# A transformer layer's seven-product matmuls: at each change of the resident operand, two blocks in turn through seven products instead of one block of eight

## The chip, the cores and the metric

One core of a Trainium2 chip runs the whole kernel. The metric is device time in microseconds (us), the median of three runs; before the change it is 2656.38 us (2653.74 to 2657.7). The engines are named as in the profile: PE (TensorE) with its weight loads PEld, DVE (VectorE), ACT (ScalarE), POOL (GpSimd), and SP (SyncE), which only issues DMAs.

## The reference: what is computed

One layer over x (2048 tokens, width 1024), all in float32:

```python
u = rms_norm(h, g_mix_pre);  z = u @ w_in            # 1024 x 2816
y = concat(swa_with_sinks(...), hgrn2(...)) @ w_out  # 1024 x 1024
h = h + rms_norm(y, g_mix_post)
y = cross_attention(rms_norm(h, g_x_pre), rms_norm(mem, g_mem), wq, wk, wv, wo)
h = h + rms_norm(y, g_x_post)
u = rms_norm(h, g_ffn_pre)
y = (silu(u @ w_gate) * (u @ w_up)) @ w_down         # 1024 x 2816 x 1024
h = h + rms_norm(y, g_ffn_post)
```

The large matrix products carry the time. Cross-attention reaches them as two of them: the query and key weights are folded into one 1024 x 1024 matrix (`qk_d`), value and output weights into another (`vo_d`).

## The kernel before, in words

**One product.** A float32 operand is kept as a rounded part and a rest (hi, lo: `split2`, L873 to L880: ACT or POOL writes hi, DVE writes lo = raw - hi). A product of a piece S (128 columns) with a resident tile T (512 columns) over `nk` slices of 128 is three matmuls for each slice, hi*hi, hi*lo, lo*hi (`products`, L1002 to L1004): 12 matmuls at nk = 4, 9 at nk = 3.

**One block.** A block is a 2x2 product of blocks: A (four pieces of 128 columns, loaded as two `sraw` tiles and split into S tiles by `streamed`) times B (four quarters, kept split as T tiles by `resident`, so that every block of a job uses the same T). It is done in one of two ways.

- `seven` (kind "s"): Strassen's way in Winograd's form. The T tiles of steps 1, 2 and 3 are quarters of B; those of steps 5, 7, 6 and 4 are differences and sums of quarters. Three S pieces of the seven are also sums (`combine`, L977, four DVE additions for a block). Three PSUM banks are used, x, y and z: x takes the products 1, 6, 7 and 4 one upon the other and is read in between (`copy`, L1017, into a `part` tile, after 1 and after 6; z is copied after 5); the outputs are x, y or z plus a copy.
- `eight` (kinds "p" and "q"): the eight plain products in four steps of two (T tiles 1, 2, 8, 3), no sums and no copies, but a T tile 8 that `seven` doesn't need.

The order of the steps stands in `STEPS` and how many S pieces each step takes in `TAKES`.

**Jobs.** A job is one B with a row of blocks; `phases` runs all jobs as one stream. The first one (`in_first`: w_in, half the tokens, 11 blocks: q, p, nine s) runs before the attention and recurrence sections, which use other code. `jobs` (L1242 on) lists the others: w_out (8 blocks), qk (8), vo (8), the FFN's gate and up products for the first half of the tokens and for the second (22 blocks each; here B is `u_d`, the normalised activations, and A the weights), and three parts of w_down (8 blocks each; nk = 3, 4, 4). At a change of job the T tiles change. `kinds` says which blocks are plain: in w_out and the first FFN job the first and the last one, in all others the last one, save that the very last block is "s": nine plain blocks in all, of which eight run behind another job or in front of one and one (w_out's first) is the start of the second part.

**The T tiles' turn.** Seven slots hold T tiles. `queue` orders them by first use; `half` starts loading half a tile (into `row` tiles of 128 x 1024, of which there are 9 for everything) when a slot's last use is past, and `split` writes the halves two products later. For qk, vo, the second FFN job and w_down the combined T's (5, 7, 6, 4) are prepared one job earlier by `combined` (L924) and stored to DRAM (`qk_s` and so on); for w_out and the first FFN job DVE combines them on the spot (L906).

**Around it.** S pieces are made two products ahead (`upto`). A block's `follow` goes on for about ten products behind it: for vo it normalises (L1439), adds the residual by an accumulating DMA issued from POOL (`add`, L1348), stores h2, squares (L1319), normalises again (L1450), transposes on PE (L1237, L1238) and stores `u_d`. Each takes one step after each product. Every tile comes from a pool with a fixed number of buffers: S 5, `raw` (the sraw tiles) 3 in the first job and 4 later, `sum` 3, `part` 3, PSUM banks for products 6. A scheduler places the instructions of each engine by its own cost estimate; each engine then runs its list in order and waits on semaphores.

Of the kernel before, what the change touches and what calls it, by code (L numbers as in the profile page):

```python
# [48 lines left out]
class Layer:  # L49
# [144 lines left out]
    def mix(self):  # L194
        tc, I = self.tc, self.I
        kw = dict(reuse_waits="tile")
        with contextlib.ExitStack() as left:
# [5 lines left out]
            with (  # L203
                tc.tile_pool(name="t1", bufs=3, **kw) as self.ts,
                tc.tile_pool(name="t2", bufs=3, **kw) as self.tb,
                tc.tile_pool(name="s1", bufs=2, side="right", **kw) as self.st_pool,
                contextlib.ExitStack() as at,
            ):
                self.banks(at, "ps1", **MOST)
                self.raws = 3  # L210
                u = self.in_first()
# [32 lines left out]
            with (  # L244
# [6 lines left out]
                self.raws = 4  # L251
# [264 lines left out]
    def in_block(self, ca, cb, beside, get, between):  # L516
# [20 lines left out]
        def out(i, j, a, b):  # L537
# [14 lines left out]
            else:  # L552
                self._n += 1
                t = self.st_pool.tile([P, 512], F32, tag="part", name=f"th_{self._n}", bufs=3)
# [315 lines left out]
    STEPS = {"s": (1, 5, 6, 3, 7, 2, 4), "p": (1, 2, 8, 3), "q": (1, 2, 8, 3)}  # L870
    TAKES = {"s": (1,) * 7, "p": (2, 2, 0, 0), "q": (4, 0, 0, 0)}
# [83 lines left out]
    def streamed(self, load, nk, kind, engine=None):  # L955
# [18 lines left out]
        def combine(a, b, op):  # L974
            self._n += 1
            t = self.st_pool.tile([P, 4, P], F32, tag="sum", name=f"sum_{self._n}", bufs=3)[:, :nk, :]
# [29 lines left out]
    def seven(self, S, T, nk, out, addend):  # L1006
# [6 lines left out]
        def copy(ps, i, j):  # L1013
            self._n += 1
            t = self.st_pool.tile([P, 512], F32, tag="part", name=f"part_{self._n}", bufs=3)
# [67 lines left out]
    def phases(self, jobs, first, prologue=None):  # L1083

        steps = [(n, i, p) for n, job in enumerate(jobs) for i, b in enumerate(job[2])
                 for p in self.STEPS[b[0]]]
        takes = [c for job in jobs for b in job[2] for c in self.TAKES[b[0]]]
        need = list(itertools.accumulate(takes)) + [sum(takes)] * 2  # L1090
# [5 lines left out]
        queue = sorted(uses, key=lambda k: (uses[k][0] - (5 if k[1] == 7 and jobs[k[0]][3] is None else 0), k))  # L1096
# [73 lines left out]
        blocks = [b for job in jobs for b in job[2]]  # L1170
        streams, ready, made = [], [], [0]

        def stream(at):
            if at < len(blocks):
                streams.append(blocks[at][1](blocks[at][0]))
                next(streams[-1])

        def upto(count):
            while made[0] < count:
                s = next(streams[0], None)  # L1180
                if s is None:
                    streams.pop(0)
                    continue
                ready.append(s)
# [9 lines left out]
        for i in range(2):  # L1194
            upto(need[i])
# [3 lines left out]
        at = 0  # L1199
        self.last = {}  # L1200
        for _, nk, bl, _, beside in jobs:
            for i, (kind, _, out, follow, addend) in enumerate(bl):
                stream(at + 1)
                after += [f() for f in beside.get(i, ())]
                run = (self.seven(ready, Ready(), nk, out, addend) if kind == "s" else
                       self.eight(ready, Ready(), nk, out, addend, kind == "q"))
                for q in range(len(self.STEPS[kind])):
                    next(run)
                    self.mark()
                    upto(need[g + 2])  # L1210
                    for _ in range(1 if kind == "s" else 2):
# [10 lines left out]
                after.append(follow())  # L1222
                at += 1
# [20 lines left out]
    def jobs(self):  # L1244
# [21 lines left out]
        def kinds(blocks, n=0):  # L1266
            return [("p" if i < n or i == len(blocks) - 1 else "s",) + b for i, b in enumerate(blocks)]
# [19 lines left out]
        jobs = [(w_out, 4, kinds([self.mixed_block(n) for n in range(0, NT, 2)], 1), None, {2: [qk_s[1]]}),  # L1287
# [302 lines left out]
```

## Time and profile before

| | |
|---|---|
| median of 3 runs | 2656.38 us (2653.74, 2656.38, 2657.7) |
| span of the profiled execution | 2652.4 us; the page has no other time of it |
| matmul instructions | 12329 |
| DVE, ACT, POOL busy | 1714.9, 1240.2, 485.2 us |
| 0 to 265 us | first job (w_in, half the tokens) |
| 265 to 815 us | w_in for the rest, attention, recurrence, folding of the cross-attention weights |
| 815 to 1010, to 1190, to 1375 us | w_out, qk, vo |
| 1375 to 2220 us | the two FFN jobs |
| 2220 to 2652 us | w_down in three parts |

The profile is one execution. A row of a timeline has start, duration, engine, line, operation, out<-in and shapes; in brackets stands how long the engine had been idle before and what released it. In a table by windows each engine has its busy time and, in brackets, its number of instructions; PEclk is the clock granted to PE. The bounds of the jobs above are read from the first and last rows of each job's tiles, to some 10 us, since neighbouring jobs overlap.

### The profile page before, as it was taken

The numbers are of one execution on the slowest core, as the hardware profiler recorded it, in microseconds if no ns is written. First come the engines' busy times: TensorE is split into PE (matmuls) and PEld (weight loads), VectorE is DVE, ScalarE is ACT, GpSimd is POOL, SyncE is SP. The second block draws the span as 40 slices with busy tenths as digits, with TensorE's granted clock in tenths as the row PEclk, the third lists the DMA queues.
The fourth block names the chain that finished last, engine by engine and source line by source line (L and its number), as shares of the span: only waits on it lengthen the run. The fifth ranks groups of instructions, "written<-read, shape, count | busy, mean of one in ns | idle before, by whom it ended". The sixth has DMA issues, their size and how long they took to land.

```text
span 2652.4 us, 34824 instructions
## 1 busy us (share of the span) xinstructions
PE 2568.9 (97%) x12329; PEld 2145.1 (81%) x12329; DVE 1714.9 (65%) x2701; ACT 1240.2 (47%) x2604; POOL 485.2 (18%) x675
## 2 busy tenths in 40 slices
PE   7999999999988999999989999999999999999998
PEld 6877888888986877888878888888888888888886
DVE  7675578877545657777666655556666656564656
ACT  5463366655433556555564333344333334353543
POOL 4240344322432323223310000000000000001022
PEclk9999999999999999999999999999999999999999
DMA  5435655445877998676893633253566435576988
GB/s 183 144 130 165 191 156 159 131 140 171 233 234 222 276 296 266 210 238 176 220 307 126 192 120 95 80 182 127 168 198 211 162 108 171 173 232 173 264 214 215
DMA packets 405102, 494.48 MB, mean 186 GB/s; under 512 B 20416, under 2 KB 311232, under 8 KB 404928
## 3 DMA queue, kind: packets, MB, share of 16 engines
q1 hardware_dynamic: 394272, 453.46, 53.3%
q0 software_dynamic: 10656, 38.80, 8.3%
q8 instruction: 97, 1.59, 0.2%
q14 instruction: 77, 0.63, 0.1%
HBM read 333.85 MB, written 158.33 MB: 186 GB/s over the span
## 4 chain that ended last, share of the span: by engine, by line
PE 75%; DMA 10%; issue 7%; DVE 4%; POOL 3%; ACT 2%; SPq 0%; POOLq 0%; DVEq 0%; ACTq 0%
PE psm L1002 20%; PE psm L1004 20%; PE psm L1003 20%; PE psg L160 2%; PE psg L159 2%; PE psg L158 2%; PE pss L1237 1%; DMA row<-y_d 1%; DMA row<-in_w_out_dram 1%; DMA u_d<-row 1%; DMA raw<-in_wv_x_dram 1%; DMA raw<-in_wo_x_dram 1%; DVE wlo L143 1%; DMA row<-in_x_dram 1%; DMA pair<-in_x_dram 0%
## 5 line engine op out<-in xcount | busy, mean ns | idle before, releaser
L1002 PE MATMUL psm<-T,S 128*128 128x512 f32 x2699 | 1049.2, 393 | 19.9 <-ACT part L1017 6.9
L1003 PE MATMUL psm<-T,S 128*128 128x512 f32 x2699 | 1054.7, 391 | 5.7 <-DVE T L880 5.7
L1004 PE MATMUL psm<-T,S 128*128 128x512 f32 x2699 | 1046.4, 392 | 0.7 <-DVE S L880 0.6
L1002 PEld LDWEIGHTS psm<-T,S 128*128 128x128 f32 x2699 | 509.3, 189 | 132.3 <-ACT part L1017 8.2
L1003 PEld LDWEIGHTS psm<-T,S 128*128 128x128 f32 x2699 | 509.3, 189 | 111.8 <-DVE T L880 7.4
L1004 PEld LDWEIGHTS psm<-T,S 128*128 128x128 f32 x2699 | 509.2, 189 | 108.9 <-DVE S L880 3.1
L880 DVE TENSOR_TENSOR S<-sraw,S 128x512 fp32r<-128x512 f32 (+1 forms) x320 | 222.9, 703 | 213.3 <-ACT S L877 195.9
L877 ACT ACTIVATE S<-sum 128x512 fp32r<-128x512 f32 (+1 forms) x310 | 186.4, 619 | 342.5 <-PE psm L1004 244.3
L880 DVE TENSOR_TENSOR S<-sum,S 128x512 fp32r<-128x512 f32 (+1 forms) x368 | 248.5, 686 | 55.4 <-ACT S L877 35.7
L1017 ACT ACTIVATE part<-psm 128x512 f32<-128x512 f32 x270 | 160.0, 597 | 245.9 <-PE psm L1004 227.9
L1348 POOL DMA_DIRECT2D row<-y_d x28 | 25.7, 918 | 1127.4 <-DVE row L1521 1033.9
L877 ACT ACTIVATE S<-sraw 128x512 fp32r<-128x512 f32 (+1 forms) x273 | 168.0, 616 | 122.7 <-PE psm L1004 102.8
L880 DVE TENSOR_TENSOR T<-row,T 128x1024 fp32r<-128x1024 f32 (+1 forms) x122 | 144.2, 1195 | 63.8 <-ACT T L877 63.6
L158 PE MATMUL psg<-u,whi 128*128 128x512 f32 x352 | 141.3, 401 | 1.6 <-POOL whi L142 1.6
L160 PE MATMUL psg<-u,wlo 128*128 128x512 f32 x352 | 139.6, 397 | 0.9 <-DVE wlo L143 0.9
L159 PE MATMUL psg<-u,whi 128*128 128x512 f32 x352 | 139.4, 396 | 0.0
L877 ACT ACTIVATE T<-row 128x1024 fp32r<-128x1024 f32 x122 | 122.3, 1028 | 33.2 <-DVE row L906 17.9
L1319 ACT ACTIVATE junk<-row 128x512 f32<-128x512 f32 x160 | 99.9, 626 | 79.1 <-DVE row L1341 28.4
L879 POOL TENSOR_SCALAR S<-sum 128x512 fp32r<-128x512 f32 x58 | 50.2, 865 | 209.8 <-PE psm L1004 159.9
L977 DVE TENSOR_TENSOR sum<-sraw,sraw 128x512 f32<-128x512 f32 (+1 forms) x92 | 64.0, 696 | 32.0 <-DMA sraw<-h1t_d 8.7
L143 DVE TENSOR_TENSOR wlo<-raw,whi 128x1024 fp32r<-128x1024 f32 x46 | 60.3, 1311 | 36.1 <-POOL whi L142 36.1
L1472 DVE TENSOR_TENSOR row<-psm,part 128x512 f32<-128x512 f32 x63 | 41.7, 688 | 59.3 <-PE psm L1004 59.2
(332 smaller groups left out, 3622.0 us busy)
## 6 DMA issues: line engine op xcount, KB each, us to landing
sraw<-in_w_gate_dram SPq DMA_DIRECT2D x44, 512.0 KB, 3.9
sraw<-in_w_up_dram SPq DMA_DIRECT2D x44, 512.0 KB, 4.0
hid_d<-row SPq DMA_DIRECT2D x44, 512.0 KB, 2.6
h_d<-row SPq DMA_DIRECT2D x32, 512.0 KB, 5.8
y_d<-row SPq DMA_DIRECT2D x32, 512.0 KB, 3.1
sraw<-hid_d SPq DMA_DIRECT2D x32, 512.0 KB, 5.3
row<-h_d POOLq DMA_DIRECT2D x30, 512.0 KB, 6.5
row<-u_d SPq DMA_DIRECT2D x30, 512.0 KB, 6.3
```

The source lines that it names most:

```text
L143: (lo_engine or nc.vector).tensor_tensor(lo, raw, f32(hi), ALU.subtract)
L158: nc.tensor.matmul(ps, ah, bh, start=(i == 0), stop=False)
L159: nc.tensor.matmul(ps, ah, bl, start=False, stop=False)
L160: nc.tensor.matmul(ps, al, bh, start=False, stop=(i == n - 1))
L877: self.nc.scalar.activation(hi, raw, AF.Copy)
L880: self.nc.vector.tensor_tensor(lo, raw, f32(hi), ALU.subtract)
L977: nc.vector.tensor_tensor(t, a, b, op)
L1002: nc.tensor.matmul(ps, s[:, 0, k, :], t[:, 0, k, :], start=st, stop=False, **kw)
L1003: nc.tensor.matmul(ps, s[:, 0, k, :], t[:, 1, k, :], start=False, stop=False, **kw)
L1004: nc.tensor.matmul(ps, s[:, 1, k, :], t[:, 0, k, :], start=False, stop=sp, **kw)
L1017: nc.scalar.activation(t, ps, AF.Copy)
L1319: self.nc.scalar.activation(junk, a, AF.Square, scale=float(D) ** -0.5, accum_out=to)
```

## The change

- A new kind "d": two neighbouring blocks go through the seven steps in turn, product by product (step 1 of the one, step 1 of the other, step 2 of the one, ...), so that each T is used twice before the next is needed. All jobs from w_out on begin and end with such a pair, save w_out's start (still one "p" block) and the end of the last job (still "s").
- The order of the seven steps is 1, 2, 5, 6, 7, 3, 4 for "s" and "d" (was 1, 5, 6, 3, 7, 2, 4), and the S pieces are made in that order.
- T tile 7, where it isn't prepared a job earlier, is fetched directly ahead of 6 (was five places early).
- Pools: `raw` 6 (was 4) and `sum` 5, `part` 4 (were 3) from the second part on. To make room in SBUF `dynamic_dma_scratch_size=2048` is given, the bytes of each partition kept for the descriptors of DMAs issued from POOL.

```diff
-    STEPS = {"s": (1, 5, 6, 3, 7, 2, 4), "p": (1, 2, 8, 3), "q": (1, 2, 8, 3)}
+    STEPS = {"s": (1, 2, 5, 6, 7, 3, 4), "d": (1, 2, 5, 6, 7, 3, 4), "p": (1, 2, 8, 3), "q": (1, 2, 8, 3)}
...
-                self.raws = 4
+                self.raws, self.parts, self.sums = 6, 4, 5
...
         yield made(a11, "A")
+        yield made(a12, "A")
         s1 = combine(a21, a22, ALU.add)
         yield made(s1, "P")
         s2 = combine(s1, a11, ALU.subtract)
         yield made(s2, "A")
+        yield made(combine(a11, a21, ALU.subtract), "P")
         yield made(combine(a12, s2, ALU.subtract), "A")
-        yield made(combine(a11, a21, ALU.subtract), "P")
-        yield made(a12, "A")
         yield made(a22, "P")
...
+                members = (i, i + 1) if job[2][i][0] == "d" else (i,)
...
-        queue = sorted(uses, key=lambda k: (uses[k][0] - (5 if k[1] == 7 and jobs[k[0]][3] is None else 0), k))
+        def turn(k):
+            if k[1] == 7 and jobs[k[0]][3] is None:
+                return uses[k[0], 5 if first else 6, 0][0] - 0.5, k
+            return uses[k][0], k
+
+        queue = sorted(uses, key=turn)
...
+            for q in range(len(self.STEPS[kind])):
+                for i in members:
+                    next(runs[i])
                     self.mark()
-                    upto(need[g + 2])
+                    upto(g + 2)
...
-        def kinds(blocks, n=0):
-            return [("p" if i < n or i == len(blocks) - 1 else "s",) + b for i, b in enumerate(blocks)]
+        def kinds(blocks, first="dd", last="dd"):
+            middle = "s" * (len(blocks) - len(first) - len(last))
+            return [(k,) + b for k, b in zip(first + middle + last, blocks)]
...
-    nc = _bacc.Bacc("TRN2", target_bir_lowering=False, num_devices=1)
+    nc = _bacc.Bacc("TRN2", target_bir_lowering=False, num_devices=1, dynamic_dma_scratch_size=2048)
```

More of the change, by code (lines that the diff above doesn't have):

```diff
@@ L975, in combine @@
             self._n += 1
-            t = self.st_pool.tile([P, 4, P], F32, tag="sum", name=f"sum_{self._n}", bufs=3)[:, :nk, :]
+            t = self.st_pool.tile([P, 4, P], F32, tag="sum", name=f"sum_{self._n}", bufs=self.sums)[:, :nk, :]
             nc.vector.tensor_tensor(t, a, b, op)
@@ L1014, in copy @@
             self._n += 1
-            t = self.st_pool.tile([P, 512], F32, tag="part", name=f"part_{self._n}", bufs=3)
+            t = self.st_pool.tile([P, 512], F32, tag="part", name=f"part_{self._n}", bufs=self.parts)
             if addend is None:
```

84 lines of the change are left out of this document (47 added, 37 removed).

## The prediction

> **What bounds the kernel now.** First the head of the page: span, engines, the clock, the chain that ended last.
>
> ```profile
> span 2652.4 us, 34824 instructions
> PE 2568.9 (97%) x12329; PEld 2145.1 (81%) x12329; DVE 1714.9 (65%) x2701; ACT 1240.2 (47%) x2604; POOL 485.2 (18%) x675
> PE 75%; DMA 10%; issue 7%; DVE 4%; POOL 3%; ACT 2%; SPq 0%; POOLq 0%; DVEq 0%; ACTq 0%
> ```
>
> PE is busy 97% of the span and makes up 75% of the chain; DVE, next, is at 65%. So time is saved by fewer matmuls or by shorter waits of PE. The span is all that the page has of the profiled execution; the median of the runs, 2656.4 us, is 4.0 above it. I reckon changes on the span and add them to 2656.4.
>
> Second the table by windows, where PE is not full (PE, PEld, DVE, ACT, POOL, then PEclk, DMA share, GB/s).
>
> ```profile
> 800.00:850.00 50.00, 41.53 (x174) 31.66 (x173) 22.73 (x23) 18.52 (x33) 8.37 (x9) 0.96 0.88 257
> 1000.00:1050.00 50.00, 44.36 (x203) 36.45 (x202) 38.93 (x53) 34.39 (x71) 15.39 (x23) 0.93 0.84 261
> 1150.00:1200.00 50.00, 49.49 (x239) 41.17 (x238) 40.96 (x66) 33.50 (x68) 11.00 (x14) 1.00 0.79 255
> 1350.00:1400.00 50.00, 42.17 (x170) 32.73 (x169) 32.89 (x35) 28.77 (x52) 5.19 (x11) 0.86 0.91 291
> 1700.00:1750.00 50.00, 50.00 (x222) 41.42 (x221) 25.60 (x39) 17.48 (x31) 0.00 (x0) 1.00 0.31 96
> ```
>
> In the FFN (1700) PE never rests and the clock is 1.00. It loses time where the resident operand changes: 800 to 850 (w_out begins), around 1000 (w_out to qk), 1350 to 1400 (vo to FFN). The last has 170 PE instructions where a full window has 222: 52 short. What one is worth, from two matmuls of a stretch without a gap, 39 apart in PE's order:
>
> ```profile
> 1599.81 0.39 PE L1004 MATMUL psm<-T,S 128*128 128x512 f32 x1
> 1608.65 0.39 PE L1004 MATMUL psm<-T,S 128*128 128x512 f32 x1
> ```
>
> 8.84 / 39 = 0.2267 us (the 0.39 is a latency, it overlaps the next). So 1350 to 1400 loses 52 x 0.2267 = 11.8 us, and 1000 to 1050 some 4.5 (19 short, and its transposes are shorter than a matmul). Third, PE's timeline at these places, with the idle time before a row and its releaser:
>
> ```profile
> 842.39 0.50 PE L1003 MATMUL psm<-T,S 128*128 128x512 f32 x1 [1.02 <-DVE T L880]
> 845.19 0.50 PE L1002 MATMUL psm<-T,S 128*128 128x512 f32 x1 [1.35 <-ACT T L877]
> 849.80 0.80 PE L1003 MATMUL psm<-T,S 128*128 128x512 f32 x1 [4.11 <-DVE T L880]
> ...
> 1003.21 1.06 PE L1237 MATMUL pss<-ident,row 128*128 128x128 f32 x8 [1.03 <-DMA row<-in_x_dram]
> 1014.37 0.90 PE L1237 MATMUL pss<-ident,row 128*128 128x128 f32 x3 [4.62 <-ACT row L1238]
> ...
> 1189.97 0.50 PE L1002 MATMUL psm<-T,S 128*128 128x512 f32 x1 [0.51 <-ACT part L1017]
> ...
> 1385.08 0.80 PE L1002 MATMUL psm<-T,S 128*128 128x512 f32 x1 [5.28 <-ACT T L877]
> 1386.46 0.79 PE L1003 MATMUL psm<-T,S 128*128 128x512 f32 x1 [0.58 <-DVE T L880]
> 1387.47 0.63 PE L1002 MATMUL psm<-T,S 128*128 128x512 f32 x1
> 1387.90 0.63 PE L1003 MATMUL psm<-T,S 128*128 128x512 f32 x1
> 1389.78 0.79 PE L1002 MATMUL psm<-T,S 128*128 128x512 f32 x1 [0.82 <-ACT row L1474]
> ```
>
> The waits are for the T tiles themselves (L877, L880), or for a copy that waits behind other work. After the 5.28 us gap matmuls start 0.43 apart (1387.47, 1387.90), twice 0.2267: the clock is halved, so 7.7 us idle become 11.8. Behind the gap at 1385 the chain shows a store and a load of u_d in series:
>
> ```profile
> 1366.44 12.38 DMA u_d<-row
> ...
> 1378.89 6.66 DMA row<-u_d
> ```
>
> **The change, part by part.** *Matmuls.* Eight plain blocks go. Seven of them have nk = 4 and give up one product of 12 matmuls, one has nk = 3 and gives up 9: 7 x 12 + 9 = 93. The built order confirms it: 8568 product matmuls where there were 8661. 93 x 0.2267 = **21.1 us**, on PE, the path. Nothing covers it.
>
> *What DVE gets for it.* The rows for the pieces:
>
> ```profile
> L880 DVE TENSOR_TENSOR S<-sum,S 128x512 fp32r<-128x512 f32 (+1 forms) x368 | 248.5, 686 | 55.4 <-ACT S L877 35.7 <-POOL S L879 17.9
> L977 DVE TENSOR_TENSOR sum<-sraw,sraw 128x512 f32<-128x512 f32 (+1 forms) x92 | 64.0, 696 | 32.0 <-DMA sraw<-h1t_d 8.7 <-DMA sraw<-in_w_in_dram 8.3 <-issue 3.4
> L1521 DVE TENSOR_TENSOR row<-psm,part 128x512 f32<-128x512 f32 x66 | 45.0, 688 | 35.5 <-PE psm L1004 35.5
> L880 DVE TENSOR_TENSOR T<-row,T 128x1024 fp32r<-128x1024 f32 (+1 forms) x122 | 144.2, 1195 | 63.8 <-ACT T L877 63.6
> L906 DVE TENSOR_TENSOR row<-row,row 128x1024 f32<-128x1024 f32 x16 | 19.6, 1225 | 15.5 <-DMA row<-in_w_out_dram 13.2 <-DMA row<-u_d 2.1
> L1439 DVE SCALAR_TENSOR_TENSOR row<-row,q_r,g 128x1024 f32<-128x1024 f32 x16 | 20.2, 1303 | 6.4 <-POOL q_r L1334 6.4
> L1450 DVE SCALAR_TENSOR_TENSOR row<-row,q_r,extra 128x1024 f32<-128x1024 f32 x16 | 20.0, 1282 | 7.2 <-POOL q_r L1334 3.7 <-DMA u_d<-row 3.5
> L1398 DVE TENSOR_REDUCE x_mx<-row 128x2 f32<-128x512 f32 x21 | 14.3, 679 | 0.1
> L1410 DVE TENSOR_SCALAR row<-row,mc 128x256 f32<-128x256 f32 x64 | 18.5, 354 | 0.3
> ```
>
> By count of instructions, DVE gets 24 more S splits, 32 more sums and 24 more outputs, at 0.69, and 16 fewer T splits at 1.2 (T tile 8 goes): 80 x 0.69 - 16 x 1.2 = +36 us over the kernel. ACT gets 24 more copies and as many S halves, less 16 T halves. Over all that is beside PE. At the changes it isn't spread. A seven-product block costs DVE 7 splits + 4 sums + 3 outputs = 14 x 0.69 = 9.7 us; a vo block adds 2 x 1.30 + 2 x 1.28 (14.8), a w_out block 2 x 1.30 (12.3), a qk block 4 x 0.68 + 8 x 0.35 (15.2); gate and up, with their product, average 11.0. A new set of T costs 14 x 1.2 = 16.7, and 8 x 1.22 = 9.8 more where DVE combines. Two pairs around a change are 28 products, 28 x 12 x 0.2267 = 76.2 us of PE. DVE's work in them: w_out to qk 24.5 + 30.4 + 16.7 = 71.6 (94%), qk to vo 30.4 + 29.6 + 16.7 = 76.7 (101%), vo to FFN 29.6 + 22.1 + 16.7 + 9.8 = 78.2 (103%). Before, with one plain block before the change (and one behind it for the FFN), the same count gives 85%, 92% and 82%. By this the pairs cost at least 0.5 us at qk to vo and 2.0 at vo to FFN. The FFN's and w_down's own changes stay under 80%: 0, hidden under PE.
>
> *When it is due.* Against that stands the order. A pair uses each T for two products, so a new T is due every 5.4 us and not every 2.7, and its slot was freed a whole pair before. I added up, in the built orders, the DVE work that stands between the S pieces of two products, less PE's time for the products between: the largest excess. At w_out's start 36.0 us before and 24.9 now; w_out to qk 14.9 and 7.6; qk to vo 12.1 and 9.3; vo to FFN 20.3 (28.5 of DVE against 8.2 of PE) and 19.0 (over 43 us of PE). Before, 12.1 went with one wait of 0.51 (1189.97), 14.9 with 4.5 lost, 20.3 with 11.8. So I take: w_out to qk -2 (half of the 4.5, for the waits there name a DMA and a copy, not T; ends -4.5 and +3.1, if its 7.6 is uncovered); qk to vo +0.5 (ends 0 and +8.8); vo to FFN 0, its excess being the same (ends -11.8 and +6.7, 18.5 uncovered for 11.8).
>
> *Order of the steps.* At w_out's start T5 and T6 are due one product (2.7 us) later, as step 2 now stands before 5 and its T is there. Of the waits 1.02, 1.35 and 4.11 at 842 to 850 that takes **2.7** (ends 0 and -6.5). In the new order 6 and 7 follow each other in the same bank, with a copy between. In the built order mostly 22 to 24 matmuls (5 us) of the next block stand between them, more than the copy needs, so 0; were they neighbours, each of the 63 single blocks behind the first job would pay a wait like the last one of the kernel, below (0.88, 55 us together). Only at the end of the first job two products meet in one bank with no matmul between, where two stood:
>
> ```profile
> 260.93 0.47 PE L1002 MATMUL psm<-T,S 128*128 128x512 f32 x1 [0.42 <-DVE pair L543]
> ...
> 2640.42 0.47 PE L1002 MATMUL psm<-T,S 128*128 128x512 f32 x1 [0.88 <-DVE row L1521]
> ```
>
> 0.88 for 0.42: **+0.5**.
>
> *Pools, DMAs.* More raw, sum and part tiles only lift waits: a pair holds up to four part tiles at once, two copies for each block, which is what there is. T tile 8 goes with 18 loads of T, four of them at vo to FFN, whose DMA share is 0.91. I take 0; what it may give there is within the ends above. The scratch for POOL's DMAs: most at once are four, by their issues and landing time:
>
> ```profile
> 2605.28 0.95 POOL L1348 DMA_DIRECT2D row<-h_d  x1 [1.62 <-DVE row L1563]
> 2607.08 0.86 POOL L1348 DMA_DIRECT2D row<-h_d  x1 [0.85 <-DVE row L1563]
> 2607.68 1.17 POOL L1348 DMA_DIRECT2D row<-y_d  x1
> 2609.58 0.86 POOL L1348 DMA_DIRECT2D row<-y_d  x1 [0.74 <-ACT row L1525]
> ...
> q0 software_dynamic: 10656, 38.80, 8.3%
> ...
> row<-h_d POOLq DMA_DIRECT2D x30, 512.0 KB, 6.5
> ```
>
> A row of this queue is 10656 / 74 issues = 144 packets, 9 on each of 16 engines, so four are 36. I take 0; if the smaller ring made one wait for another's landing, 6.5 us at each such place, mostly beside w_down, where POOL has nothing else.
>
> Sum: -21.1 - 2.7 - 2 + 0.5 + 0 + 0.5 = -24.8; 2656.4 - 24.8 = **2632 us**.
>
> [...]
>
> **Rivals.** *A, the changes get smooth.* For it: each of the four excesses falls, and four loads fewer where DMA is at 0.91. Then w_out to qk gives 4.5, vo to FFN keeps its 2.0 of overflow and gives 9.8: -21.1 - 2.7 - 4.5 + 0.5 - 9.8 + 0.5 = -37, 2619 us. Against it: DVE at 101 and 103%.
>
> *B, row tiles at vo to FFN.* The last two vo blocks now end together and hold 4 y and 4 u rows, 8 of the 9 buffers, when the FFN's T's and outputs want theirs. The pair of rows above (12.38 + 6.66) is such a row coming free. For it: that is what ended the 5.28 gap; against: T's are fetched earlier than the u rows are taken. Once more it is 19.0 us, with the halved clock some 23: -24.8 + 23, 2655 us, no difference.
>
> *C, slower: DVE becomes the bound at the three changes.* Place: w_out to qk, qk to vo, vo to FFN. Price: the excesses uncovered, 7.6 + 9.3 + 18.5 = 35.4 us idle, by the 11.8 / 7.7 of 1385 54 with the halved clock, less 16.8 lost there now: +37. With -21.1 - 2.7 + 0.5 it is +14, 2670 us. It decides from where the three changes lose 23 us more than now. For it: 94 to 103%; against: the excess fell, and before, at 1150 to 1200, DVE's 40.96 of 50 us left PE 49.49.
>
> *D, nothing is saved*, because the pairs are pulled apart or the matmuls stay: excluded by the count of 8568.
>
> **How the numbers follow.** Forecast (2625 to 2645) 0.48; A (below 2625) 0.18; B (2645 to 2662) 0.18; C (above 2662) 0.14; 0.02 elsewhere. The measurement can tell 0.2%, 5.3 us, from no change. Faster, below 2651.1: 0.48 + 0.18 + half of B and the rest, 0.76; the same, to 2661.7: 0.10; slower: 0.14. Range: from the middle of A to the upper part of B, 2614 to 2657, which leaves C and the ends out.
>
> **What would show it.** In the profile after: 2668 matmuls on each of L1002 to L1004's lines for psm<-T,S, and PE busy some 20 us less. At w_out's start a last wait of 1 to 2 us in place of 4.11. The windows of the changes at 210 PE instructions or more and PEclk 1.00 speak for A; waits of PE on DVE T or DVE S at all three changes, DVE at 45 of 50 us, for C; a wait there that ends with a load of u_d behind a store, for B. I am wrong in the main if new waits of PE show within the FFN or w_down, which I cost at nothing.

## The result, and the profile after

The changed kernel takes 2650.72 us (median of 20 runs, 2643.26 to 2655.48) against 2656.59 us (20 runs, 2649.47 to 2665.44): a ratio of **0.9979, 95% interval 0.9970 to 0.9988**, 5.6 us less by the ratio. The forecast was 24.8 us less, 2632 us; the range, 2614 to 2657, holds the time. So some 19 us of the forecast gain are missing.

The head of the page of the changed kernel (span and engines) and one of the three lines of the products' matmuls:

```profile
span 2653.7 us, 34559 instructions
PE 2548.9 (96%) x12236; PEld 2126.5 (80%) x12236; DVE 1747.7 (66%) x2765; ACT 1241.9 (47%) x2624; POOL 488.0 (18%) x675
...
L1002 PE MATMUL psm<-T,S 128*128 128x512 f32 x2668 | 1039.3, 394 | 43.3 <-ACT part L1017 13.2
```

2668 instead of 2699, and PE is busy 20.0 us less (2568.9 before): the matmuls went as forecast. But the span isn't shorter, so PE's idle time grew by as much and 1.3 us more. This execution took 2655.48 us, the longest of the 20; a second profile, of run e8 below, is of one of 2647.06 us (span 2645.3). What both show I take for the kernel's, and the rest for scatter. The table by windows of the first (columns as in the prediction):

```profile
850.00:900.00 50.00, 36.32 (x142) 28.37 (x141) 36.50 (x42) 22.83 (x45) 13.75 (x19) 0.80 0.73 191
...
1150.00:1200.00 50.00, 50.00 (x230) 41.51 (x230) 42.01 (x70) 34.05 (x75) 13.97 (x19) 1.00 0.62 200
...
1350.00:1400.00 50.00, 41.62 (x183) 33.52 (x182) 42.47 (x50) 31.21 (x61) 13.45 (x16) 0.94 0.93 291
...
1700.00:1750.00 50.00, 50.00 (x222) 41.39 (x222) 28.08 (x44) 17.14 (x30) 0.00 (x0) 1.00 0.23 75
```

Inside the FFN PE is as full as before, and at 1150 to 1200, where DVE has 42 of 50 us, too. The new hole is 850 to 900, at the start of w_out: 142 instructions, clock 0.80 (before, that window had 227). PE's timeline there, and behind vo, with the idle time ahead of a row:

```profile
820.34 0.79 PE L1002 MATMUL psm<-T,S 128*128 128x512 f32 x1 [5.80 <-POOL S L879]
859.85 0.79 PE L1002 MATMUL psm<-T,S 128*128 128x512 f32 x1 [7.50 <-ACT T L877]
866.23 1.97 PE L1257 MATMUL pss<-ident,row 128*128 128x128 f32 x8 [4.64 <-DMA row<-in_x_dram]
...
954.10 0.76 PE L1002 MATMUL psm<-T,S 128*128 128x512 f32 x1 [4.10 <-DVE row L1361]
...
1344.32 0.50 PE L1002 MATMUL psm<-T,S 128*128 128x512 f32 x1 [2.36 <-ACT S L877]
...
1391.83 0.50 PE L1002 MATMUL psm<-T,S 128*128 128x512 f32 x1 [2.48 <-ACT part L1017]
1396.41 0.80 PE L1004 MATMUL psm<-T,S 128*128 128x512 f32 x1 [3.84 <-DVE S L880]
```

To see where the time went I measure each job in PE's timeline from the start of its first product matmul to the start of the next job's, and the last part of w_down to the start of the last product matmul. Where a job ends is found by counting: w_out has 684 product matmuls (696 before), qk and vo 672 (684), the FFN jobs 1848 (1872, 1860), w_down 504, 672, 672 (513, 684, 672). The first row goes from the span's start to the first matmul of w_in for the second half of the tokens, the second from there to w_out. All in us:

| | before | changed, 1st profile | 2nd profile | forecast change | change, 2nd |
|---|---|---|---|---|---|
| first job | 265.6 | 268.9 | 265.0 | +0.5 | -0.5 |
| to w_out's first product | 550.9 | 551.5 | 547.6 | 0 | -3.3 |
| w_out | 187.6 | 199.0 | 198.7 | -5.4 | **+11.2** |
| qk | 178.9 | 172.7 | 172.1 | -4.7 | -6.9 |
| vo | 169.2 | 173.1 | 172.5 | -2.2 | **+3.3** |
| FFN 1 | 441.6 | 434.7 | 436.8 | -5.4 | -4.9 |
| FFN 2 | 421.6 | 418.9 | 418.9 | -2.7 | -2.7 |
| w_down, first two parts | 271.3 | 266.6 | 266.6 | -4.8 | -4.8 |
| w_down, third part | 156.3 | 159.5 | 158.2 | 0 | **+1.9** |

(The forecast column is the prediction's sum laid out by job, 2.72 us for each block of 12 matmuls. Of the kernel before there is one profile; run e12 below, which differs from it in the scratch alone, has the same times to 2.1 us.) In FFN 2 and the first parts of w_down, where the matmuls are all that the sum changes, the forecast is right to 0.1 us. The loss stands in w_out with what leads to it (13 us off), vo (5.5 us) and the last part of w_down (2 to 3 us).

### The profile page after: what moved, and what is told of

Read it like the earlier page. It is cut to its first block, busy times and chain, and to the rows that moved or that the text cites. A ratio compares the mean times of both kernels' runs of the same rounds, so it can differ in the third digit from the quotient of the medians.

```text
span 2653.7 us, 34559 instructions
## 1 busy us (share of the span) xinstructions
PE 2548.9 (96%) x12236; PEld 2126.5 (80%) x12236; DVE 1747.7 (66%) x2765; ACT 1241.9 (47%) x2624; POOL 488.0 (18%) x675
## 4 chain that ended last, share of the span: by engine, by line
PE 73%; DMA 11%; DVE 6%; issue 3%; POOL 3%; ACT 2%; SPq 0%; POOLq 0%; DVEq 0%; ACTq 0%
PE psm L1002 20%; PE psm L1004 20%; PE psm L1003 20%; PE psg L160 2%; PE psg L159 2%; PE psg L158 2%; DMA row<-in_x_dram 1%; PE pss L1257 1%; DVE S L880 1%; DMA row<-u_d 1%; DMA row<-in_w_down_dram 1%; DMA z<-in_w_out_dram 1%; DMA row<-qk_s 1%; DVE T L880 1%; POOL whi L142 1%
## 5 line engine op out<-in xcount | busy, mean ns | idle before, releaser
L1002 PEld LDWEIGHTS psm<-T,S 128*128 128x128 f32 x2668 | 504.2, 189 | 155.6 <-ACT part L1017 16.5
L1004 PEld LDWEIGHTS psm<-T,S 128*128 128x128 f32 x2668 | 503.2, 189 | 117.0 <-DVE S L880 12.5
L1003 PEld LDWEIGHTS psm<-T,S 128*128 128x128 f32 x2668 | 504.1, 189 | 105.8 <-DVE T L880 2.5
L877 ACT ACTIVATE S<-sum 128x512 fp32r<-128x512 f32 (+1 forms) x336 | 206.9, 619 | 342.9 <-PE psm L1004 331.7
L880 DVE TENSOR_TENSOR S<-sraw,S 128x512 fp32r<-128x512 f32 (+1 forms) x312 | 211.4, 684 | 227.6 <-ACT S L877 207.6
L880 DVE TENSOR_TENSOR S<-sum,S 128x512 fp32r<-128x512 f32 (+1 forms) x400 | 274.3, 689 | 69.3 <-ACT S L877 57.5
L1017 ACT ACTIVATE part<-psm 128x512 f32<-128x512 f32 x294 | 173.3, 593 | 170.3 <-PE psm L1004 168.2
L1339 ACT ACTIVATE junk<-row 128x512 f32<-128x512 f32 x160 | 99.7, 625 | 112.8 <-DMA row<-in_x_dram 35.1
L880 DVE TENSOR_TENSOR T<-row,T 128x1024 fp32r<-128x1024 f32 x106 | 127.2, 1205 | 33.4 <-ACT T L877 33.0
L877 ACT ACTIVATE T<-row 128x1024 fp32r<-128x1024 f32 x106 | 108.1, 1029 | 59.2 <-DVE row L906 32.5
L1501 DVE TENSOR_TENSOR part<-psm,part 128x512 f32<-128x512 f32 x66 | 45.4, 688 | 63.4 <-PE psm L1004 63.3
```

The lines of the kernel that those rows point to most:

```text
L877: self.nc.scalar.activation(hi, raw, AF.Copy)
L880: self.nc.vector.tensor_tensor(lo, raw, f32(hi), ALU.subtract)
L1002: nc.tensor.matmul(ps, s[:, 0, k, :], t[:, 0, k, :], start=st, stop=False, **kw)
L1003: nc.tensor.matmul(ps, s[:, 0, k, :], t[:, 1, k, :], start=False, stop=False, **kw)
L1004: nc.tensor.matmul(ps, s[:, 1, k, :], t[:, 0, k, :], start=False, stop=sp, **kw)
L1017: nc.scalar.activation(t, ps, AF.Copy)
```

## The experiments

**Theories.** P: the larger pools cost it, by delaying the loads at the start of w_out. O: the new order of the steps costs it. D: the pairs overload DVE at the changes (the prediction's rival C). Below, "us" beside a ratio is (ratio - 1) x 2655.

### The parts of the change by themselves

e1, the pools: to the kernel before only

```diff
-                self.raws = 4
+                self.raws, self.parts, self.sums = 6, 4, 5
-    num_devices=1)
+    num_devices=1, dynamic_dma_scratch_size=2048)
```

> The kernel before, with only the larger pools (raw 6, sum 5, part 4 from the second part on) and the smaller scratch; steps, order and plain blocks as before. Theory P (larger pools delay the start of w_out: the six raw tiles take SBUF in which tiles of the middle part still lie, so the first loads of y_d wait behind the last stores of vo_d, and four more loads of y_d stand ahead of w_out's T rows in SP's queue): slower than before by 10 to 13 us, ratio 1.004 to 1.005, with PE waits of 5 us or more in 815 to 870 us. Theory O (the new step order costs it) and theory D (the pairs overload DVE at the changes): no difference, ratio 1.000 within 0.001, the waits at the start of w_out as before (6.5 us).

Measured: **1.0049** (1.0035 to 1.0062), +13.0 us. As P has it in size, but only in part in place: the waits at w_out's start are there (5.79 and 3.91 us), yet up to the end of w_out (first job left out) this run takes just 3.7 us more than before; vo takes 4.9 us more, the third part of w_down 4.1.

e2, the order: to the kernel before only the new `STEPS`, the S pieces in that order, and `turn`.

> The kernel before, with only the new step order 1, 2, 5, 6, 7, 3, 4 (S pieces in that order, T7 fetched directly ahead of 6, or of 5 in the first job); pools and plain blocks as before. Theory O: the first job gets some 3 to 4 us longer (products 6 and 7 meet in one bank behind a copy), and the start of w_out and the single blocks lose too: slower by 5 to 15 us, ratio 1.002 to 1.006. Theory P: only the first job's 3 to 4 us show, and w_out's start gains the 2.7 us of the prediction: ratio 1.000 to 1.001. Theory D: as P.

Measured: **1.0089** (1.0075 to 1.0104), +23.6 us, more than any theory gave. The first job isn't it (265.0 us, before 265.6). By the table's measure w_out takes 203.3 us (+15.7), vo 178.7 (+9.5), w_down's third part 160.0 (+3.7). PE's timeline of this run has waits for T's and copies at w_out's start, where the forecast took 2.7 us off, and behind every change, where before stood 4.62, 0.51 and 5.28:

```profile
849.62 0.49 PE L1002 MATMUL psm<-T,S 128*128 128x512 f32 x1 [3.81 <-ACT part L1017]
853.66 0.80 PE L1003 MATMUL psm<-T,S 128*128 128x512 f32 x1 [3.55 <-DVE T L880]
...
1031.52 0.80 PE L1003 MATMUL psm<-T,S 128*128 128x512 f32 x1 [2.64 <-DVE T L880]
...
1226.60 0.50 PE L1002 MATMUL psm<-T,S 128*128 128x512 f32 x1 [2.54 <-ACT T L877]
...
1410.70 0.80 PE L1002 MATMUL psm<-T,S 128*128 128x512 f32 x1 [5.01 <-ACT row L1479]
```

e5, order and pools, all of the change but the pairs:

> The kernel before with the new step order and the larger pools with the smaller scratch, but with the plain blocks instead of pairs: all of the change save the pairs. Theory 1 (the pairs bring all of their 21 us, and order and pools together take some 15 of them): slower than before by 15 us, ratio 1.005 to 1.007. Theory 2 (the pairs themselves wait for DVE and bring a few us only): within 5 us of before, ratio 0.999 to 1.002. If the effects of order (23 us) and pools (13 us) simply added, it would be 36 us slower, ratio 1.014, which the changed kernel with 21 us of matmuls less (ratio 0.998) speaks against.

Measured: **1.0122** (1.0100 to 1.0145), +32.4 us: order and pools nearly add. So the pairs bring (0.9979 - 1.0122) x 2655 = **-38 us** (half-width 6, from the two intervals), not the 21 of their matmuls. By jobs against e5 (w_out 204.0, qk 181.5, vo 180.9, FFN 1 439.1), the second profile has 5.2, 9.4, 8.4 and 2.4 us less, where the matmuls give 2.7, 2.7, 2.7 and 5.4. So at w_out to qk and qk to vo the pairs give time, and D is out there. At vo to FFN they give no more than their matmuls; what holds PE there is taken up with e16 and e17.

e7 and e9 ask the same with the old order. In the old order a pair holds six part tiles, so both have raw 5, part 6, sum 5; e7 has pairs (and the change's later fetch of T tile 7, which e9 hasn't), e9 is the kernel before with those pools.

```diff
-    STEPS = {"s": (1, 2, 5, 6, 7, 3, 4), "d": (1, 2, 5, 6, 7, 3, 4),
+    STEPS = {"s": (1, 5, 6, 3, 7, 2, 4), "d": (1, 5, 6, 3, 7, 2, 4),
-                self.raws, self.parts, self.sums = 6, 4, 5
+                self.raws, self.parts, self.sums = 5, 6, 5
```

> The changed kernel with the old step order 1, 5, 6, 3, 7, 2, 4 for pairs and single blocks, and raw 5, sum 5, part 6 (in the old order a pair holds up to six part tiles at once). If the new order is what costs (23.6 us by itself with the old pools), this is faster than the raw 5 run by 10 us or more, ratio to before 0.990 to 0.993. If the order costs only where sum and part tiles are few, the same as the raw 5 run within 3 us.

> The kernel before with raw 5, sum 5, part 6 and the smaller scratch: what the pairs in the old order stand on, without the pairs. If the pairs give just their matmuls (8 products, 21 us) in the old order, this is slower than before by 12 us, ratio 1.0045 (the pairs in the old order had 0.9967, 9 us faster). If five raw tiles lose little, it is 1.000 to 1.002, and the pairs then give only 9 to 13 us in the old order.

Measured: e7 **0.9967** (0.9956 to 0.9978), e9 **1.0076** (1.0062 to 1.0089). The pairs give (0.9967 - 1.0076) x 2655 = -29 us (half-width 5) here. e9 costs 20 us, more than either branch of its expectation. e7's -8.8 us is within 4 us of the changed kernel and within 3 of e6 below, which has raw 5 and the new order. So with pairs the order makes little difference, where without them it cost 24 us (e2) or 19 (e5 less e1). Why the T's come late without pairs is located by e2's rows, not settled.

Which pool costs: e10 raw 6 alone, e11 sum 5 and part 4 alone, e12 the scratch alone (the first two with the scratch).

> The kernel before with raw 6 (was 4) and the smaller scratch; sum and part stay 3. If the 13 us that the larger pools cost (ratio 1.0049) come from the six raw tiles, by SP's queue: ratio 1.004 to 1.005, a wait of some 6 us for POOL S at the first product of w_out and one of 4 us or more for T behind it. If from sum and part: 1.000 to 1.001.

> The kernel before with sum 5, part 4 (were 3) and the smaller scratch; raw stays 4. If the 13 us come from the raw tiles: 1.000 within 0.001. If more sum and part tiles let the scheduler put DVE's work in another order (the built order of DVE differs in many places) and that costs: 1.003 to 1.005, with PE waits on DVE row and ACT row behind w_out.

> The kernel before with the smaller scratch for POOL's DMAs alone; the order of the instructions is nearly the same. By the prediction 0: ratio 1.000 within 0.001. If the smaller ring makes one DMA of POOL wait for another, the last part of w_down, where POOL issues 58 of them, gets 4 to 5 us longer: ratio 1.0015 to 1.002.

Measured: e10 1.0017 (1.0007 to 1.0027), e11 **1.0041** (1.0027 to 1.0054), e12 0.9997 (0.9988 to 1.0007). The scratch costs nothing that these runs can tell. Raw 6 costs 4.5 us, with the waits expected or nearly (5.70 and 3.86 us at w_out's start). Most comes from sum and part, which no run takes apart. P was right on the sum and wrong on the share. DVE's line for the first sum of a block, of e11:

```profile
L977 DVE TENSOR_TENSOR sum<-sraw,sraw 128x512 f32<-128x512 f32 (+1 forms) x92 | 64.0, 695 | 133.2 <-DMA sraw<-hid_d 37.4 <-DMA sraw<-in_w_up_dram 32.8 <-DMA sraw<-in_w_gate_dram 21.9
```

The same line of the kernel before, in the prediction, has 32.0 us of idle time ahead of it; here it is 133.2. In DVE's list for the third part of w_down the first sum of a block now stands ahead of the last two outputs of the block before, where it stood behind all three, and comes before its raw tiles have landed. In those 133.2 us DVE stands idle, with outputs and S pieces behind the sums in its list: the third part takes 165.0 us (+8.7) in e11. The idle time in the FFN costs nothing (FFN 2 takes 421.6 us, as before).

With six raw tiles this standing is gone: in e1 the line has 33.5 us, and 0.1 in the third part of w_down; in the changed kernel 5.2. So it explains e11, and e3 below, but not the 13.0 us of e1. There PE's waits in the third part are for DVE's outputs (1.83 and 1.41 us for L1521); their cause stays open.

### Around the changed kernel

e3 and e6 take the changed kernel with raw 4 and raw 5, e4 with the old order in the first job alone, e8 is the changed kernel again.

> The changed kernel with raw 4 in place of 6 (sum 5, part 4, pairs, order and scratch as changed). Theory P: w_out's start gets back what it lost, 10 to 13 us faster than the changed kernel, ratio to before 0.993 to 0.994, and the first y_d loads stand ahead of the vo_d stores again; if a pair needs the two more raw tiles later, single waits of PE on S pieces come at the pairs. Theories O and D: as the changed kernel, ratio 0.998, or slower.

> The changed kernel with raw 5 in place of 6. In the order of SP's queue the first loads of y_d then stand ahead of the vo_d stores again, and only one more load of y_d stands ahead of w_out's second T rows. If it is the queue's order at the start of w_out that costs the 10 us between raw 6 and raw 4 there, and if the lost time of raw 4 in the last part of w_down comes from raw tiles that are too few, this run has the one without the other: faster than the changed kernel by 5 to 10 us, ratio to before 0.994 to 0.996. If a pair needs six, it loses in the last part of w_down as raw 4 did: ratio 0.999 to 1.001.

> The changed kernel with the old step order (and the old early fetch of T7) in the first job alone. If the order costs the first job 3 to 4 us, as the two profiles show (the next part begins at 268.9 us and not 265.6), it is that much faster than the changed kernel: ratio to before 0.9965 to 0.997. All theories agree on the first job; they part on the rest, which this run leaves as it is. If the 3.3 us are scatter of one execution: 0.998.

> The changed kernel once more, for a second profile beside the first, which is of the longest of its 20 runs. The waits at the start of w_out (5.8 and 7.5 us in the first profile) and at the end of vo (2.4, 2.1, 2.5, 3.8 us) come again within 1 to 2 us if they lie in the order of the queues; the first job's 3.3 us don't, as three other kernels with the new order in it show 265.0 to 265.4 us for the first job. Ratio 0.997 to 0.999.

Measured: e3 1.0014 (1.0002 to 1.0026), e6 0.9975 (0.9963 to 0.9987), e4 0.9982 (0.9972 to 0.9993), e8 0.9985 (0.9973 to 0.9997). e4: the first job's 3.3 us are scatter; the eleven other profiles with the new order in it have 264.0 to 267.5. e8: the waits of w_out and vo come again. e3 and e6 part two effects of the raw tiles. Up to the end of w_out (first job left out) raw 4 takes 740.0 us and raw 5 741.2, the changed kernel 750.5 and 746.4: six tiles cost 5 to 10 us there. But in w_down's third part raw 4 takes 169.6 us, raw 5 155.8. Even so raw 5 is not the 5 to 10 us faster that was expected: its FFN 1 takes 439.5 us, with a wait of 5.95 us for a copy at 1392.76. The line of the first sum in that part (window 2490 to 2660), raw 4:

```profile
L977 DVE TENSOR_TENSOR sum<-sraw,sraw 128x512 f32<-128x512 f32 x6 | 4.1, 691 | 37.6 <-DMA sraw<-hid_d 37.6
```

37.6 us in which DVE stands for loads; the changed kernel has 0.1. So five sum tiles need more than four raw tiles.

What six raw tiles do at the start of w_out is seen on SP's timeline, which lists the loads in the order of its queue. Before:

```profile
820.80 3.62 SPq L75 DMA_DIRECT2D row<-in_w_out_dram  x6
824.52 0.54 SPq L75 DMA_DIRECT2D extra<-qk_d  x1
825.10 15.75 SPq L75 DMA_DIRECT2D row<-in_w_out_dram  x12
```

And changed:

```profile
814.71 1.38 SPq L75 DMA_DIRECT2D sraw<-y_d  x2
...
818.18 9.89 SPq L75 DMA_DIRECT2D row<-in_w_out_dram  x8
828.49 4.03 SPq L75 DMA_DIRECT2D sraw<-y_d  x4
832.83 2.93 SPq L75 DMA_DIRECT2D extra<-qk_d  x1
835.87 0.54 SPq L75 DMA_DIRECT2D sraw<-y_d  x1
836.46 17.26 SPq L75 DMA_DIRECT2D row<-in_w_out_dram  x12
```

Five loads of y_d, for w_out's third block and those behind it, have slipped ahead of the rows for w_out's next T's; the second set of rows starts 11.4 us later (836.46 for 825.10; w_out's first product itself starts 3.9 later). And w_out's very first loads of y_d, which before had been issued long ahead (their row stands at 765.06), come at 814.71, behind stores of vo_d: hence the 5.80 for POOL S, which comes with raw 6 in e1 and e10 too and is absent with raw 4 and 5 (e3, e6). The waits behind it are not the raw tiles' alone: with raw 4 there are still 4.05 us for a copy and 2.52 for a T, and 4.84 for row<-in_x_dram.

### Instructions that stand at the head of a queue

e13 puts w_out's T rows first; nothing else changes.

```diff
+                    with contextlib.ExitStack() as behind:
+                        if not first and 2 <= at <= 4:
+                            traced = self.nc.cur_bb.bb.instructions
+                            behind.enter_context(self.tc.issue_after(
+                                next(x for x in reversed(traced) if x.engine == mybir.EngineType.SP)))
-                    next(streams[n, i])
+                        next(streams[n, i])
```

> The changed kernel, with the loads of y_d for the third to fifth group of w_out's blocks held behind the last load traced before them, so that w_out's T rows stand ahead of them in SP's queue; nothing else changed, raw 6. If the place in SP's queue is what makes the T's late at the start of w_out (waits of 7.5 and 6.8 us there in the two profiles of the changed kernel): that wait falls to 2 us or less, w_out with what comes before it is 5 to 8 us shorter, ratio to before 0.995 to 0.996. If the DMA engines are simply full there, the T's come as late as before: 0.998.

Measured: 0.9977 (0.9965 to 0.9990), no gain over the changed kernel. PE's timeline in this run:

```profile
845.62 0.49 PE L1002 MATMUL psm<-T,S 128*128 128x512 f32 x1 [1.14 <-ACT part L1017]
848.76 0.79 PE L1003 MATMUL psm<-T,S 128*128 128x512 f32 x1 [2.64 <-DVE T L880]
...
914.28 0.79 PE L1004 MATMUL psm<-T,S 128*128 128x512 f32 x1 [4.23 <-DVE S L880]
```

The wait for T falls from 7.50 to 2.64, with 1.14 for a copy ahead of it: the place in the queue was the cause of about half, and the rest, above the 2 us expected, stays. But the S pieces whose loads were held back are now late (4.23 at 914), and w_out takes 200.6 us: given back further on.

e14 looks at vo. The squares (L1339) of a block's follow wait on ACT for an accumulating DMA, with S and T pieces behind them, as in ACT's row ahead of PE's wait of 2.36 at 1344 in the changed kernel. (From e15 on the lines behind 1194 stand 5 or 6 further down: L1344 is the square, L1373 the issue of the accumulating DMA.)

```profile
1340.50 0.63 ACT L1339 ACTIVATE junk<-row 128x512 f32<-128x512 f32 x1 [4.65 <-DMA row<-h_d]
```

In this edit and those of e17 and e18 `n` counts tiles of 128 tokens, two to a block: the "last four blocks" of the expectations are the two blocks of the job's last pair.

```diff
-            yield
+            for _ in range(3 if n < NT - 4 else 1):
+                yield
             for i in range(2):
                 self.mean_squares(y[i], i, s2)
```

> The changed kernel, with the squares that follow a vo block two products later (for all blocks of vo but the last four), so that ACT doesn't reach them before the accumulating DMA has landed. If PE's waits of 2.3 and 0.6 us at the last pair of vo come from ACT standing at a square that waits for row<-h_d, with the S and T pieces behind it in ACT's queue: both waits go, 3 us faster than the changed kernel, ratio 0.997. If those S pieces are late for DVE's load: no difference, 0.998.

Measured: 1.0017 (1.0007 to 1.0028), 10 us slower than the changed kernel. The wait of 2.36 at vo's last pair is gone, but three others of 1.0 to 1.6 us came inside vo, which takes 174.9 us, and FFN 1 now waits 4.32 us for a T. How the edit leads there stays open:

```profile
1285.24 0.50 PE L1002 MATMUL psm<-T,S 128*128 128x512 f32 x1 [1.57 <-ACT part L1017]
...
1389.55 1.22 PE L1002 MATMUL psm<-T,S 128*128 128x512 f32 x2 [4.32 <-ACT T L877]
```

e15 and e16 have raw 5, e13's edit, and four products in place of three between the load of qk_d and the DVE operation that takes it; e15 has e14's edit as well. The reason for the third edit is DVE's row ahead of the wait at 954.10 in the changed kernel: DVE stands 8.01 us at this operation, and the output that frees PE's bank (953.27, L1361) is behind it.

```profile
951.52 1.23 DVE L924 TENSOR_TENSOR extra<-extra,row 128x1024 f32<-128x1024 f32 x1 [8.01 <-DMA extra<-qk_d]
```

> The changed kernel with what the runs so far point to together: raw 5, w_out's T rows ahead of further loads of y_d, four products in place of three between the load of qk_d and the DVE operation that takes it (3.8 to 4.3 us of waits near 945 us, where DVE stands at that operation), and the squares behind vo two products later. Each mechanism gives its waits: 5 + 4 + 3 us on top of the changed kernel's 0.998, ratio 0.993 to 0.994. If the waits only move to the next DMA in a queue: 0.996 to 0.998.

> The changed kernel with raw 5, w_out's T rows ahead of further loads of y_d, and four products between the load of qk_d and its DVE operation; the squares behind vo as in the changed kernel. The run with the later squares showed the part up to the end of w_out 9 to 12 us shorter than in the changed kernel, and lost 2 us in vo and 8 to 13 us in the first FFN job. If those losses come from the later squares alone: ratio to before 0.9945 to 0.9955, w_out with what comes before it 738 to 740 us, the first FFN job 435 to 439 us. If they come from raw 5 or from the rest: 0.998.

Measured: e15 0.9986 (0.9977 to 0.9996), e16 **0.9962** (0.9950 to 0.9974). Both fall short of what was hoped (0.993 to 0.994, and 0.9945 to 0.9955, into which e16's interval reaches). Up to the end of w_out e15 takes 737.8 us and e16 737.4, 9 to 13 less than the changed kernel and some 4 less than raw 5 alone (e6), and no wait above 1 us is left near 950. e15 loses it again in FFN 1 (448.4 us) by the later squares, e16 less so (440.9). What is left there, in e16: PE's wait, ACT's row ahead of the copy that PE waits for, POOL's rows, and the window.

```profile
1391.89 0.79 PE L1002 MATMUL psm<-T,S 128*128 128x512 f32 x1 [7.94 <-ACT part L1017]
```

```profile
1388.93 0.63 ACT L1344 ACTIVATE junk<-row 128x512 f32<-128x512 f32 x1 [7.00 <-DMA row<-h_d]
```

```profile
1377.38 3.60 POOL L1355 TENSOR_TENSOR q_v<-q_s 128x2 f32<-128x2 f32 x1 [3.90 <-ACT junk L1344]
1380.94 0.88 POOL L1373 DMA_DIRECT2D row<-h_d  x1
```

```profile
1350.00:1400.00 50.00, 37.77 (x142) 29.28 (x141) 41.26 (x50) 28.02 (x55) 16.47 (x16) 0.83 0.81 234
```

Read from below: POOL waits at q_v for squares of the one block of the pair, and the accumulating DMA of the other is issued behind it; ACT reaches the square that needs this DMA early and stands there 7.00 us; PE's copy is behind the square. Two follows in step share three queues, and each makes the other wait. Nothing of ACT's list passes the square in those 7.00 us.

e17 is e16 with the squares two products later in vo's last pair alone, whose `u_d` rows only the second FFN job reads.

```diff
-            yield
+            for _ in range(1 if n < NT - 4 else 3):
+                yield
```

> The kernel of the run before (raw 5, w_out's T rows first, four products at qk_d), with the squares behind the last four blocks of vo two products later. In the run before ACT stood 7.0 us at such a square, for the accumulating DMA row<-h_d, which POOL issued late behind a step of the other block of the pair; a part copy stood behind the square, and PE waited 7.94 us for it at the start of the first FFN job. If that head of ACT's queue is the cause, the wait falls to 2 us or less and the run is 4 to 6 us faster than the run before: ratio to before 0.994 to 0.995, the first FFN job 435 us. If the row tiles, held longer, or DVE take its place: 0.996 to 0.998.

Measured: **0.9939** (0.9922 to 0.9955), 16.2 us faster than before and 6 than e16; FFN 1 takes 430.4 us, 10.5 less than in e16. The longest wait behind vo is 1.55 us, the clock stays at 1.00, and the window has 200 instructions:

```profile
1372.38 0.50 PE L1003 MATMUL psm<-T,S 128*128 128x512 f32 x1 [1.40 <-DVE T L880]
...
1383.97 0.50 PE L1002 MATMUL psm<-T,S 128*128 128x512 f32 x1 [1.55 <-ACT part L1017]
```

```profile
1350.00:1400.00 50.00, 44.45 (x200) 34.81 (x199) 47.05 (x59) 35.27 (x68) 14.41 (x16) 1.00 0.86 254
```

So at vo to FFN the head of ACT's queue it was. DVE has 47 of 50 us in this window, and PE none the less waits no longer than 1.55 us: the bound that rival C spoke of isn't reached here either. Within vo a wait of 2.42 us and one of 1.94 remain, and vo takes 173.8 us.

e18 makes the same edit in w_out's last pair as well.

> The kernel of the run before, with the same edit also in w_out: the squares behind its last four blocks two products later. In the run before PE waits 4.67 us for a part copy at the start of qk, and ACT's rows ahead of that copy are squares that waited for row<-in_x_dram (3.67, 1.51, 2.00 us). If the head of ACT's queue is the cause here as behind vo: that wait falls to 2 us or less and the run is 2 to 4 us faster than the run before, ratio to before 0.992 to 0.993. If it only moves, as with the earlier vo blocks: 0.994 or above.

Measured: **0.9926** (0.9912 to 0.9941), 2632.64 us, 19.6 us faster than before; against e17 the intervals overlap. The wait at the start of qk went from 4.67 (e17) to 2.20, but 0.77 and 1.25 us for DVE S came beside it, so here the wait mostly moved:

```profile
1023.51 0.50 PE L1004 MATMUL psm<-T,S 128*128 128x512 f32 x1 [1.25 <-DVE S L880]
...
1029.62 0.50 PE L1002 MATMUL psm<-T,S 128*128 128x512 f32 x1 [2.20 <-ACT S L877]
1031.12 0.79 PE L1004 MATMUL psm<-T,S 128*128 128x512 f32 x1 [0.77 <-DVE S L880]
```

## Why the prediction was right and wrong

- **Matmuls, -21.1: right.** x2668 on each line, PE busy 20.0 us less, 2.7 us for each block where nothing else changed.
- **Pools, "I take 0": wrong.** They cost the kernel before 13.0 us (e1). Its scratch part was right (e12: 0). "More raw, sum and part tiles only lift waits" is the sentence that failed: a free buffer lets the scheduler place an instruction earlier in an in-order list, ahead of others that are due sooner. For the raw tiles this is shown (the SP rows: y_d ahead of T rows; 5 to 10 us up to the end of w_out in the changed kernel; e16, which also moves the T rows and the operation on qk_d, gets back 9 to 13 there). For sum and part it is shown only with four raw tiles (e11: DVE stands 133 us for loads); what they cost beside six is measured and not explained. The built orders that I counted excesses in showed such places; I counted DVE's work between pieces and not the DMA that the piece at the head waits for.
- **Order of the steps, -2.7 and +0.5: wrong, and by these runs the largest step that failed.** By itself it costs 23.6 us (e2), on top of the pools 19 (e5 less e1). The -2.7 at w_out's start became waits of 5.80, 7.50 and 4.64. Of these the 5.80 is the raw tiles' (e10), and the place in the queue made half of the 7.50 (e13); but the order alone, with the old pools, has 3.81, 3.55 and 3.54 there (e2). That step 2 gives T5 and T6 a product's time more was right; that they and the copies would then be in time was not, and why they are late stays open. With pairs the old order is just 2 to 3 us faster (e7), which the intervals don't tell from 0. The +0.5 in the first job can't be told from 0 (e4).
- **Changes, w_out to qk -2, qk to vo +0.5, vo to FFN 0: too small a gain.** The pairs bring 29 to 38 us, 8 to 17 beyond their matmuls, and by jobs that lies at w_out to qk and qk to vo. It is a gain over kernels that order or pools had slowed at just these places; over the kernel before only qk clearly gains more than its matmuls (6.9 us). The falling excesses, which I took for half of a 4.5, had the right sign. In the sum: -38 (pairs) + 32.4 (order and pools, e5) gives the -5.6, which is no test, since the -38 is the difference of the two.
- **vo:** it lost 3.3 us instead of gaining 2.2. I had named DVE and the row tiles; the rows show ACT, standing 4.65 us at a square for an accumulating DMA, and with the squares later that wait is gone (e14). But vo gets no faster by it: it takes 172 to 175 us in nearly every run with pairs, so its loss is located and not cured. The same at the head of ACT's queue behind vo cost FFN 1 some 10 us in e16 (e17). The rows of the two follows, which a pair puts in step, should have been laid out on ACT and POOL as I did for DVE.
- **FFN and w_down, 0:** right within the FFN; the third part of w_down is 1.9 to 3.2 us longer, as e1 (+4.1) and e2 (+3.7) have it without pairs.
- **Rivals:** C fell (pairs gain at two of its three changes, at the third e17 runs with DVE at 47 of 50 us, and at 1150 to 1200 PE is full). B's time (2655) came near by another cause: the wait of 3.84 at 1396 goes back to a load of u_d, but in the chain of the changed kernel that load alone takes the time (row below), with no store ahead of it. A's smooth change at vo to FFN came true only in e17 and e18.

```profile
1380.41 13.49 DMA row<-u_d
```

- **The gap:** the prediction saw the halved clock behind a wait of 5.28 us and priced rival C by it (11.8 us for 7.7). It came behind a shorter one too: one of 1.83 us in e1 (last section). The forecast's sum doesn't use it.

## What to carry to other kernels

Before a buffer count is raised, look in the built order at what moves ahead in each in-order list, SP's too, and ask for every instruction that now comes earlier which DMA it waits for and what stands behind it. Price an edit's parts separately: here pairs (-38), order and pools (+32) nearly cancel, and the small net change hides large ones. A wait that names a copy or an S piece is followed back to the row ahead of it on that engine; the fix that paid was to move the waiting instruction later (e17), where nobody soon needs its result; at the other blocks the same move cost time (e14).

## What the runs showed of the hardware

The clock was halved behind a wait far shorter than the 5.28 us of the prediction, and late. In e1 the wait is 1.83 us: the next matmuls start 0.23 apart, and only from 1.4 us later on 0.43 apart.

```profile
2572.89 0.50 PE L1002 MATMUL psm<-T,S 128*128 128x512 f32 x1 [1.83 <-DVE row L1521]
...
2573.22 0.39 PE L1003 MATMUL psm<-T,S 128*128 128x512 f32 x1
2573.45 0.39 PE L1004 MATMUL psm<-T,S 128*128 128x512 f32 x1
...
2574.26 0.63 PE L1004 MATMUL psm<-T,S 128*128 128x512 f32 x1
2574.69 0.63 PE L1002 MATMUL psm<-T,S 128*128 128x512 f32 x1
```

In e13 a longer one, 2.77 us, left the clock at 1.00 in the windows below:

```profile
1377.10 0.50 PE L1003 MATMUL psm<-T,S 128*128 128x512 f32 x1 [2.77 <-DVE T L880]
```

In the clock records of the kernel before and of the changed one 19 stretches of halved clock are whole (the cut-off end of each trace left out): 11 last 3.41 us, 6 last 6.83, one 13.65 and one 17.07. Windows of 3.41 us around the two waits, first e1, then e13 (columns as in the prediction):

```profile
2570.59:2574.00 3.41, 1.58 (x8) 0.98 (x7) 3.41 (x6) 0.00 (x0) 2.03 (x3) 1.00 0.49 74
2574.00:2577.41 3.41, 3.41 (x10) 2.63 (x9) 3.13 (x6) 0.00 (x0) 0.67 (x1) 0.50 1.06 203
...
1372.77:1376.18 3.41, 1.55 (x7) 0.94 (x5) 3.41 (x5) 2.62 (x6) 1.83 (x2) 1.00 0.98 235
1376.18:1379.59 3.41, 2.49 (x11) 2.08 (x12) 3.41 (x4) 0.69 (x3) 0.00 (x1) 1.00 1.06 282
```

The 1.83 us of e1 lie in one window, and the granted clock is 0.50 in the next; the 2.77 of e13 fall into two (1.86 and 0.92), and it is 1.00 in both. So of these two waits the longer one is not the one with the halved clock behind it; what decides between them is not settled here.
